# Loading x, the tables and the positions from ScalarE's DMA queue instead of SyncE's

## The chip, the core and the metric

The kernel runs on one core of a Trainium2 chip. Times are device microseconds (us) of that core; lower is better. TensorE is PE, VectorE is DVE, ScalarE is ACT, GpSimd is POOL, SyncE is SP. In the profile, PEld is PE's weight load, and SPq stands for transfers that SP issues.

## What is computed

Two layers of an encoder over 256 tokens of width 1024, all in float32. Each layer has a mixer sub-layer and an expert sub-layer, each behind an RMS norm that is scaled and shifted by a vector computed from the conditioning input c:

```python
cond = jax.nn.silu(c)
for l in range(DEPTH):
    mod = cond @ w_ada[l] + b_ada[l]
    sh1, sc1, gt1, sh2, sc2, gt2 = jnp.split(mod[:, None, :], 6, axis=-1)
    h = rms_norm(x, g_norm1[l]) * (1 + sc1) + sh1
    x = x + gt1 * hybrid_mixer(h, pos, w_in[l], ...)
    h = rms_norm(x, g_norm2[l]) * (1 + sc2) + sh2
    x = x + gt2 * hier_moe(h, w_gr[l], b_gr[l], w_er[l], b_er[l], w1[l], w3[l], w2[l])
return x
```

The mixer projects h once (`w_in`, 6944 columns), runs three kinds of attention on parts of the result, and merges them. The positions `pos` enter through rotary angles and distances between tokens. The expert sub-layer sends each token to 2 of 32 experts.

## The kernel before

**Stages.** `run` (L128) calls `plan`, which writes down the order of all weight loads, then `setup`, then the generators of the two layers: mixer, experts, mixer, experts. Instructions of an engine run in the order in which the program emits them; nothing reorders them (a manual schedule).

**Weights.** All large weights come through a stream: `plan` (L190) fills a deque of transfers, and `pump` (L73) issues the next ones from SP into buffers of 128 x 12 KB, as long as fewer than `ring` (6 here) weights are held ready and one of the 10 buffers is free in the program's order. Most weights fill a buffer with 1536 KB. The first in the stream are three parts of the first modulation matrix, `('ada', 0, 0, 0)` to `('ada', 0, 0, 2)` (called `ada 0`, `ada 1`, `ada 2` here; the third is 1024 KB), then the first halves of the first three slices of `w_in`, then `ada 3` to `ada 5`, and so on. `pump(n)` stops when n weights are held. `Tile` semaphores make a transfer wait, at issue, for an earlier transfer that used the same semaphore, and for the last reader of its buffer.

**Setup.** `setup` (L237) starts with everything that is needed early. On ACT: the load of the activation table for Exp and Ln (L240). On SP, in this order: `pk` (L242: the conditioning input, selectors, gains and an identity matrix, 98 KB), `rows` (L248: tables and short vectors, one row of 1456 bytes read for each of the 128 partitions), `ipos` (L252: positions, 1032 bytes a partition), the two tiles of x (L254, 128 rows of 4 KB each), and with `pump(2)` `ada 0` and `ada 1` (L85). Then two biases `bz` behind DVE's memsets (L258, L259), and further weights by `pump(4)`, `load_kr` (L281) and `pump()`. From `pk` ACT and DVE compute `cond` = silu(c) (L272 to L276), which every `ada` matmul reads.

**The order behind it.** The first mixer emits, for layer 0 (L1245): `setup_late` (L287), then the first step of the generator `ada_half(0)`, which is `ada 0` on PE (12 matmuls, 4 side by side on 32 columns of PE each), then `norm_x` (L481), then 16 transposes of the normed x on PE (L1254), then the rest of `ada_half(0)`: `ada 1`, `ada 2`, the bias (L435), transposed into columns (`modab`, L445). `setup_late` is work on DVE and ACT: positions to floats (L300 to L302), angles, sine and cosine (L309 to L320), gains (L326 to L334), rope tables (L343). `norm_x` sums squares of x, the left halves on ACT (L477), the right halves on DVE (L492), takes the root (L108 to L115) and scales x to `xn` (L501 on ACT, L503 on DVE). With `modab`, DVE and ACT scale the transposes and split them into two parts, `hH` and `hL` (L1281, L1286, L1287); the first projection (`in`) on PE starts on `hH`. Only then does the mixer proper begin; `ada 3` to `ada 5` and the right half of h come later in it, and the masks, a triangle and router weights are loaded from POOL's queue (L353, L354, L285).

Of the kernel before, what the change touches and what calls it, by code (L numbers as in the profile page):

```python
# [22 lines left out]
EXP_LN = 'natural_log_exp_and_others'  # L23
# [14 lines left out]
class Kern:  # L38
# [198 lines left out]
    def setup(self):  # L237

        nc, a, C = self.nc, self.a, self.const
        nc.scalar.preload_act_table_set(EXP_LN)  # L240
        pk = C('pk', [128, N_PK])
        nc.sync.dma_start(pk, a['pk'])  # L242
        self.ccol, self.sel4, self.cols = pk[:, 0:8], pk[:, 8:12], pk[:, 12:68].rearrange("p (l n) -> p l n", l=DEPTH)
        self.ident = pk[:, 68:196]
        self.identb = C('identb', [128, 128], BF)
        self.x = [self.alloc('w', [128, D], F32, 'x') for _ in range(2)]
        self.rows = C('rows', [128, N_ROW + DEPTH * 108])
        nc.sync.dma_start(self.rows, bass.AP(tensor=a['rows'].tensor, offset=a['rows'].offset,  # L248
                                             ap=[[0, 128], [1, N_ROW + DEPTH * 108]]))
        self.lrow = self.rows[:, N_ROW:].rearrange("p (l n) -> p l n", l=DEPTH)  # L250
        self.ipos = self.alloc('s', [128, 2 + T], I32, 'ipos')
        nc.sync.dma_start(self.ipos, a['pos'])  # L252
        for t in range(2):
            nc.sync.dma_start(self.x[t], a['x'][t])  # L254
        self.pump(2)
        self.bz0 = [self.alloc('s', [128, 512], F32, 'bz') for _ in range(2)]
        for h in range(2):
            nc.vector.memset(self.bz0[h], 0.0)  # L258
            nc.sync.dma_start(self.bz0[h][0:64:32], a['b_ada'][0, 0][h::2])  # L259
        self.sel2 = C('sel2', [128, 2])  # L260
        nc.vector.tensor_add(self.sel2, self.sel4[:, 0:2], self.sel4[:, 2:4])
        self.pump(4)
        self.load_kr(0)
        self.pump()
        nc.vector.tensor_copy(self.identb, self.ident)
        self.eps = C('eps', [128, 1])
        nc.vector.memset(self.eps, EPS)
        self.zero = C('zero', [128, 1])
        nc.vector.memset(self.zero, 0.0)

        t1 = self.small(8)
        nc.scalar.activation(t1, self.ccol, AF.Exp, scale=-1.0)  # L272
        nc.vector.tensor_scalar(t1, t1, 1.0, None, op0=ALU.add)
        nc.vector.reciprocal(t1, t1)
        self.cond = C('cond', [128, 8])
        nc.vector.tensor_mul(self.cond, t1, self.ccol)  # L276
        self.mod = {}
# [1636 lines left out]
```

## Time and profile before

| what | us |
|---|---|
| median of 3 runs | 1406.43 (1405.89 to 1408.21) |
| the profiled execution | 1407.64 |
| its span in the trace | 1405.5 |
| PE / DVE / ACT / POOL busy in it | 1336.0 / 683.4 / 537.3 / 187.7 |

The profile covers one execution. A span is cut into stretches by time; times in it count from the span's start. A duration of an instruction is its own; "idle before" is how long its engine stood idle ahead of it, with the work whose end released it. PE's matmuls are pipelined, so PE shows as busy while the next matmul follows; how fast it runs is read from how many matmuls fit into a time.

### The profile page before, as it was taken

Reading aid. Unit: us, or ns where it says so; the run is one execution under the profiler, and the core shown is the slowest. Engines: PE = TensorE matmul, PEld = TensorE weight load, DVE = VectorE, ACT = ScalarE, POOL = GpSimd, SP = SyncE. Lnnn points to the kernel's source line nnn. Section 1 sums busy time; section 2 is a strip of 40 time slices with the busy share of each in tenths; the row PEclk is TensorE's granted clock in tenths of the full one; section 3 lists DMA queues with packets and bytes.
Section 4 is the critical chain, followed back from the end, with each engine's and each line's share of the span. In section 5 each row is a group of like instructions: output and inputs, shape, how many; then the busy total and the mean of one; then the engine's idle time right before and its main releaser. Section 6 shows DMA issues by size and latency. Waiting matters only on the chain. (4 is left out here: it accounts for less than half of the span.)

```text
span 1405.5 us, 19475 instructions
## 1 busy us (share of the span) xinstructions
PE 1336.0 (95%) x7662; PEld 877.6 (62%) x7662; DVE 683.4 (49%) x1404; ACT 537.3 (38%) x1134; POOL 187.7 (13%) x170
## 2 busy tenths in 40 slices
PE   5999999998899999999899999999889999999997
PEld 3778787887544444444368988888764444444443
DVE  5587564767623323332256775566863233233222
ACT  4555553563422222221155555456433222222211
POOL 0002064325100000000000203540810000000000
PEclk9999999999999999999999999999899999999999
DMA  9865557267689999999994526516767999999993
GB/s 375 365 248 212 196 211 291 99 270 280 232 348 427 425 425 425 425 425 425 420 414 160 203 90 259 176 76 254 270 239 289 405 425 426 425 425 426 424 424 129
DMA packets 45215, 437.95 MB, mean 312 GB/s; under 512 B 5080, under 2 KB 5608, under 8 KB 11328
## 3 DMA queue, kind: packets, MB, share of 16 engines
q1 hardware_dynamic: 44832, 435.78, 76.5%
q8 instruction: 62, 1.02, 0.3%
q0 software_dynamic: 288, 0.89, 0.2%
q14 instruction: 33, 0.27, 0.1%
HBM read 435.59 MB, written 1.05 MB: 311 GB/s over the span
## 5 line engine op out<-in xcount | busy, mean ns | idle before, releaser
L102 PE MATMUL in<-h,hH 128*128 128x384 f32 (+1 forms) x576 | 206.1, 358 | 3.7 <-ACT hH L1286 2.5
L1631 DVE TENSOR_TENSOR O<-O,gth 64x512 f32<-64x512 f32 (+1 forms) x132 | 88.8, 673 | 241.0 <-PE O L102 240.0
L102 PE MATMUL in<-h,hL 128*128 128x384 f32 (+1 forms) x576 | 195.3, 339 | 0.1
L102 PE MATMUL in<-l,hH 128*128 128x384 f32 (+1 forms) x576 | 194.6, 338 | 0.0
L1570 ACT ACTIVATE u<-A 64x384 f32<-64x384 f32 x64 | 31.1, 486 | 301.2 <-PE A L102 301.2
L102 PEld LDWEIGHTS in<-h,hH 128*128 128x128 f32 x576 | 109.1, 189 | 29.3 <-issue 18.0
L102 PEld LDWEIGHTS in<-h,hL 128*128 128x128 f32 x576 | 108.9, 189 | 1.4 <-DVE hL L1287 1.3
L102 PEld LDWEIGHTS in<-l,hH 128*128 128x128 f32 x576 | 109.3, 190 | 0.5
L1520 ACT ACTIVATE xT<-ga,modab 128x128 f32<-128x128 f32 x256 | 92.8, 467 | 21.0 <-PE ga L102 20.9
L1637 ACT ACTIVATE Op<-O 128x1024 fp32r<-128x1024 f32 x30 | 31.7, 1057 | 138.7 <-DVE O L1631 138.7
L1571 DVE SCALAR_TENSOR_TENSOR u<-A,m,u 64x384 f32<-64x384 f32 x64 | 39.4, 616 | 89.9 <-ACT u L1570 86.2
L743 POOL TENSOR_TENSOR rot<-TB,rope 128x256 f32<-128x256 f32 x8 | 11.7, 1483 | 488.4 <-ACT UC L813 429.0
L102 PE MATMUL ga<-Poh,xp 128*128 128x256 f32 x512 | 71.7, 295 | 0.0
L1540 DVE CAST PTp<-PTe 128x256 fp32r<-128x256 bf16 x32 | 13.6, 425 | 117.4 <-PE PTe L102 117.4
L102 PE MATMUL y<-Op,PTp 128*128 128x512 f32 x240 | 70.2, 415 | 0.0
L102 PEld LDWEIGHTS ga<-Poh,xp 128*128 128x128 f32 x512 | 66.0, 198 | 5.8 <-issue 4.4
L887 ACT ACTIVATE P<-P,m 128x256 f32<-128x256 f32 (+1 forms) x48 | 27.6, 576 | 79.2 <-DVE m L945 37.1
L102 PEld LDWEIGHTS y<-Op,PTp 128*128 128x128 f32 x240 | 40.6, 188 | 21.1 <-issue 15.5
L1638 DVE TENSOR_TENSOR Op<-O,Op 128x1024 fp32r<-128x1024 f32 x30 | 36.8, 1225 | 33.8 <-ACT Op L1637 29.2
L970 POOL TENSOR_SCALAR qz<-UC,gq 128x384 f32<-128x384 f32 x16 | 22.7, 1417 | 142.7 <-PE oT L102 72.6
L973 POOL TENSOR_SCALAR bias<-dist 128x128 f32<-128x128 f32 (+1 forms) x48 | 36.1, 752 | 5.2 <-PE oT L102 1.3
L102 PE MATMUL br<-kh,oA 128*128 128x512 f32 x96 | 31.3, 401 | 0.0
(845 smaller groups left out, 2532.3 us busy)
## 6 DMA issues: line engine op xcount, KB each, us to landing
piece<-in_w_e SPq DMA_DIRECT2D x12, 512.0 KB, 4.1
w('ada', 0, 0, 0)_4_90<-in_w_ada SPq DMA_DIRECT2D x1, 1536.0 KB, 9.5
w('ada', 0, 0, 1)_5_92<-in_w_ada SPq DMA_DIRECT2D x1, 1536.0 KB
w('in', 0, 0)_9_104<-in_w_in SPq DMA_DIRECT2D x2, 768.0 KB, 16.4
w('in', 0, 1)_10_108<-in_w_in SPq DMA_DIRECT2D x2, 768.0 KB, 16.3
w('in', 0, 2)_11_110<-in_w_in SPq DMA_DIRECT2D x2, 768.0 KB, 12.2
w('ada', 0, 0, 3)_18_194<-in_w_ada SPq DMA_DIRECT2D x1, 1536.0 KB
w('ada', 0, 0, 4)_35_250<-in_w_ada SPq DMA_DIRECT2D x1, 1536.0 KB
```

The source lines that it names most:

```text
L102: self.nc.tensor.matmul(out, lhsT, rhs, start=start, stop=stop)
L743: g.tensor_mul(t[i], x, tab[:, i, :, None, :].to_broadcast([128, 2, nh, 16]))
L887: nc.scalar.activation(dst, src, AF.Exp, bias=mx_neg[:, i:i + 1], scale=1.0, accum_out=sm[:, i:i + 1])
L970: nc.gpsimd.tensor_scalar(qz, M['qd'][:, pr::2, t * 128:t * 128 + 128], self.gq[:, l, 1 + hh:2 + hh], None, op0=ALU.mult)
L973: nc.gpsimd.tensor_scalar(bias[:, lo:hi], self.dist[:, t, 256 + lo:256 + hi], -DIL_SLOPE[g][h], None, op0=ALU.mult)
L1520: nc.scalar.activation(dst, src, AF.Identity, scale=a2[:, kt:kt + 1], bias=s2[:, kt:kt + 1])
L1540: V.tensor_copy(PT[p], pv)
L1570: nc.scalar.activation(u[b:b + 64], A[c:c + 64, :384], AF.Silu)
L1571: V.scalar_tensor_tensor(u[b:b + 64], A[b:b + 64, :384], GC[e // 2][b:b + 64, e % 2:e % 2 + 1], u[b:b + 64], op0=ALU.mult, op1=ALU.mult)
L1631: V.tensor_mul(O[e // 2][b:b + 64, 512 * h + c:512 * h + c + n], o[c][p, :n], gt[p, c:c + n])
L1637: nc.scalar.activation(hi, whole, AF.Copy)
L1638: V.tensor_sub(lo, whole, hi)
```

## The change

The four transfers of x, `rows` and `ipos` are issued by ACT instead of SP, x first. `pump(2)`, the first two weights, stands directly behind `pk` on SP. The table load of ACT moves behind its four transfers.

```diff
     def setup(self):
 
         nc, a, C = self.nc, self.a, self.const
-        nc.scalar.preload_act_table_set(EXP_LN)
         pk = C('pk', [128, N_PK])
         nc.sync.dma_start(pk, a['pk'])
         self.ccol, self.sel4, self.cols = pk[:, 0:8], pk[:, 8:12], pk[:, 12:68].rearrange("p (l n) -> p l n", l=DEPTH)
         self.ident = pk[:, 68:196]
         self.identb = C('identb', [128, 128], BF)
         self.x = [self.alloc('w', [128, D], F32, 'x') for _ in range(2)]
+        for t in range(2):
+            nc.scalar.dma_start(self.x[t], a['x'][t])
+        self.pump(2)
         self.rows = C('rows', [128, N_ROW + DEPTH * 108])
-        nc.sync.dma_start(self.rows, bass.AP(tensor=a['rows'].tensor, offset=a['rows'].offset,
+        nc.scalar.dma_start(self.rows, bass.AP(tensor=a['rows'].tensor, offset=a['rows'].offset,
                                              ap=[[0, 128], [1, N_ROW + DEPTH * 108]]))
         self.lrow = self.rows[:, N_ROW:].rearrange("p (l n) -> p l n", l=DEPTH)
         self.ipos = self.alloc('s', [128, 2 + T], I32, 'ipos')
-        nc.sync.dma_start(self.ipos, a['pos'])
-        for t in range(2):
-            nc.sync.dma_start(self.x[t], a['x'][t])
-        self.pump(2)
+        nc.scalar.dma_start(self.ipos, a['pos'])
+        nc.scalar.preload_act_table_set(EXP_LN)
         self.bz0 = [self.alloc('s', [128, 512], F32, 'bz') for _ in range(2)]
```

## Rows read from the trace of the kernel before

**Rows 1.** The page, its first line.

```profile
span 1405.5 us, 19475 instructions
```

**Rows 2.** Busy time by stretch: its length, engines (instructions), granted clock, DMA, GB/s.

```profile
0.00:25.57 25.57, 10.05 (x56) 4.53 (x56) 13.99 (x72) 9.80 (x18) 0.36 (x5) 0.98 0.91 359
...
60.00:420.00 360.00, 345.38 (x2006) 269.57 (x2007) 231.31 (x498) 171.69 (x360) 93.48 (x82) 0.98 0.62 237
420.00:735.00 315.00, 304.51 (x1752) 149.16 (x1749) 100.56 (x170) 85.19 (x186) 0.00 (x0) 0.99 1.01 425
```

**Rows 3.** Waits of SP's queue, 60 to 420: total, times, longest.

```profile
SPq L85 <- DVE l L584: 104.6, 9, 19.9
SPq L85 <- PE ada L102: 60.1, 11, 14.6
```

**Rows 4.** Timeline of the start-up: start, us, engine, line, what [idle before, releaser].

```profile
6.07 0.17 DVE L300 TENSOR_SCALAR ci<-ipos 128x2 int32<-128x2 int32 x1 [2.42 <-DMA ipos<-in_pos]
...
12.68 0.68 DVE L492 SCALAR_TENSOR_TENSOR junk<-x 128x512 f32<-128x512 f32 x1
...
12.71 3.63 PE L102 MATMUL ada<-w('ada', 0, 0, 0)_4_90,cond 128*32 128x512 f32 x12 [12.71 <-DMA w('ada', 0, 0, 0)_4_90<-in_w_ada]
...
16.31 0.18 PEld L1254 LDWEIGHTS trx<-pk,xn 128*128 128x128 f32 x1 [1.70 <-DVE xn L503]
...
18.94 1.48 PE L102 MATMUL ada<-w('ada', 0, 0, 1)_5_92,cond 128*32 128x512 f32 x10
...
25.57 0.69 PE L102 MATMUL in<-h,hH 128*128 128x384 f32 x1 [2.02 <-ACT hH L1286]
```

**Rows 5.** The same timeline: what ACT and SP's queue start in front of that.

```profile
0.73 1.28 ACT L240 ACT_TABLE_LOAD   x1 [0.73 <-PEq L1902]
...
1.65 0.43 SPq L252 DMA_DIRECT2D ipos<-in_pos  x1
...
2.80 0.21 ACT L272 ACTIVATE m<-pk 128x8 f32<-128x8 f32 x1 [0.78 <-DMA pk<-in_pk]
...
3.08 0.44 SPq L85 DMA_DIRECT2D w('ada', 0, 0, 0)_4_90<-in_w_ada  x1
...
5.53 0.39 SPq L85 DMA_DIRECT2D w('ada', 0, 0, 2)_8_102<-in_w_ada  x1
```

**Rows 6.** Transfers issued 0 to 60: count, KB each, us from issue to landing.

```profile
w('ada', 0, 0, 0)_4_90<-in_w_ada SPq DMA_DIRECT2D x1, 1536.0 KB, 9.5
w('ada', 0, 0, 1)_5_92<-in_w_ada SPq DMA_DIRECT2D x1, 1536.0 KB
...
x<-in_x SPq DMA_DIRECT2D x2, 512.0 KB, 6.0
w('ada', 0, 0, 2)_8_102<-in_w_ada SPq DMA_DIRECT2D x1, 1024.0 KB, 13.2
...
rows<-in_rows SPq DMA_DIRECT2D x1, 182.0 KB, 3.6
...
ipos<-in_pos SPq DMA_DIRECT2D x1, 129.0 KB, 4.4
...
pk<-in_pk SPq DMA_DIRECT2D x1, 98.0 KB
```

**Rows 7.** DMA queues, 48 to 53.5: packets, MB, share (q1 SP, q0 POOL).

```profile
q1 hardware_dynamic: 157, 1.73, 78.1%
q0 software_dynamic: 152, 0.50, 22.7%
```

**Rows 8.** Busy time by stretch, columns as in rows 2: the transfers' first stretches.

```profile
2.00:7.20 5.20, 0.00 (x0) 0.00 (x0) 1.85 (x13) 1.51 (x3) 0.00 (x0) 1.00 0.86 279
7.20:16.30 9.10, 3.58 (x12) 0.67 (x12) 7.50 (x51) 4.11 (x10) 0.00 (x0) 1.00 1.01 416
```

**Rows 9.** PE's rate: transposes `trx` by stretch, `ada 3` (groups, 37 to 39.2), first projection.

```profile
16.30:17.62 1.32, 1.31 (x6) 1.10 (x7) 0.00 (x0) 0.00 (x0) 1.00 0.99 417
17.62:18.94 1.32, 1.32 (x12) 1.15 (x11) 0.33 (x1) 0.00 (x0) 1.00 0.99 407
...
L102 PE MATMUL ada<-w('ada', 0, 0, 3)_18_194,cond 128*32 128x512 f32 x12 | 1.9, 600 | 0.0
...
25.57:31.34 5.77, 5.77 (x18) 5.47 (x19) 4.90 (x9) 5.33 (x10) 0.00 (x0) 0.50 1.00 422
```

## The prediction

> **What bounds the kernel now.** I began with the page for the span [rows 1] and then cut the span into stretches [rows 2]: PE works nearly without a gap from 25.57 us to the end, and 25.57 us at the front are a start-up in which it works for only 10.05. In the mixer stage (60 to 420) the DMA engines move 237 GB/s, and the waits of SP's queue say why: it holds a weight back until DVE or PE has released a buffer [rows 3]. In the expert stage that follows PE and the DMA engines are both full, at 425 GB/s [rows 2], on weights whose buffers came free in the same way. So nothing behind the start-up runs on a timetable of its own: what comes later at 25.57 us comes later at the end, by the same amount, and what comes earlier likewise.
>
> The question is therefore which chain ends last in the start-up. The timeline gives two [rows 4]. One is the weight `ada 0`: PE starts on it at 12.71, when it lands, and its 12 matmuls take 3.63, to 16.34. The other starts at the positions: DVE's L300 waits for `ipos` until 6.07; behind it, in program order, stands all of `setup_late` (angles, gains, rope tables) up to 12.68, where DVE first touches x (L492). The norm follows, and the transposes start at 16.31, released by DVE's `xn`. The two chains meet within 0.03 us. Behind them PE runs in order: 16 transposes, `ada 1` and `ada 2` from 18.94, and the first projection at 25.57. DVE shows no idle time in front of L492: **the x chain is the positions' landing plus 10.24 us of fixed work**, and it is the one that the change moves later.
>
> **The change, part by part.**
>
> *The weights.* `ada 0` is issued at 3.08 now, behind pk, rows, ipos and two x [rows 5]. Afterwards it is SP's second transfer, at about 1.2. If it shares the DMA engines evenly with x, pk, both x tiles and `ada 0` are 98 + 1024 + 1536 = 2658 KB [rows 6], 2.72 MB, at 416 GB/s [rows 8] 6.5 us; from 2.0, where the transfers begin, it lands near 8.6 to 9.0. PE does its 12 matmuls some 3.8 us earlier. Worth: 0, because the transposes behind them on PE wait for `xn`, and the weights' chain had no more than its own 0.03 us to give.
>
> *x.* It lands 6.0 us after its issue, and DVE first reads it at 12.68 [rows 4, 6]. An earlier x is worth 0: DVE and ACT come to it only after the positions' work.
>
> *Table load and the four issues on ACT.* Four issues of some 0.43 us stand ahead of a table load of 1.28 [rows 5], so the Exp of L272 moves from 2.80 to about 4.0, by when pk has landed too, now sharing with x. `cond` follows a few short instructions later, about 5; its first reader is `ada 0` on PE, at 8.6 or later. Worth 0, hidden by that transfer; without this cover it would cost the 1.2 by which the Exp is later. SP saves four issues; its later ones (bz, `ada 2` now issued at 5.53) come earlier, and no queue of POOL is touched.
>
> *The positions.* This is the term that counts. Before, they were third in the only queue in use and landed in 4.4 us [rows 5, 6]. Now they are fourth in ACT's queue, and SP's queue is full of weights beside it. What two queues do to each other is seen later in this trace, where POOL loads the masks and tables beside SP's weights: between 48 and 53.5 us the one queue got 152 packets through and the other 157, though SP's carried 1.73 MB and POOL's 0.50 [rows 7]. **They take turns packet by packet, whatever their size.** All these transfers (but bz) cover 128 partitions with one row each, so they have equally many packets, and the turns pair them: pk with x 0, `ada 0` with x 1, `ada 1` with rows, `ada 2` with ipos. When ipos has had its last turn, all eight are nearly through: 98 + 1536 + 1536 + 1024 + 1024 + 182 + 129 = 5529 KB, 5.66 MB [rows 6]; at 416 GB/s 13.6 us, from 2.0 to 15.6, and a little for the slower first microsecond: 16.0. That is 9.9 later than 6.07.
>
> The bounds of it: ACT's queue served ahead of SP's would bring the positions at 2.0 + 1433 KB / 416 GB/s = 5.5 (0.5 earlier); shares equal by bytes at 2.0 + 6.8 = 8.8 (2.7 later: 98 + 2 x 1335 KB); and if the early stretch were as slow as it is now (279 GB/s, 2.0 to 7.2) the same set would be through when it is now, with `ada 2` at 5.53 + 13.2 = 18.7 (12.7 later) [rows 5, 6, 8]. I take 16.0: the row with two queues side by side is the nearest.
>
> *What else moves.* The transposes then start at 16.31 + 9.9 = 26.2. PE has been idle since its `ada 0` ended near 12.6. The first work after an idle start runs at half rate here: 12 `ada 0` matmuls in 3.63 us, the same 12 of `ada 3` in 1.9 [rows 4, 9]; and of the transposes, 6 fit into the first 1.32 us and 12 into the next [rows 9]. The granted clock prints 1.00 over both, so I go by the durations. Before, `ada 0` paid for this; afterwards the transposes and one or two of the five groups of `ada 1` and `ada 2` do. PE ran at full rate from about 17.6, 4.9 us after its first work at 12.71. At six to 1.32 us all 16 transposes take 3.5 us instead of 2.64: +0.8. That leaves 1.4 us of slow `ada` work, two groups of four matmuls; three such groups cost 1.7 more when slow, the last one's run-out included, so some 0.4 each: another 0.8. Together **+1.6**, with 0 and +2.9 (all five groups slow) as ends.
>
> The first projection now starts at a granted clock of 0.50, the 1.2 GHz level, which lasts from 25.57 to 31.34 [rows 9] and follows an idle PE, its last 2.02 us spent on ACT's `hH` [rows 4]. That gap moves along, so I leave the low stretch where it is relative to the work: 0. If it stayed away, 18 matmuls would take half of 5.77: -2.9.
>
> The sum: 9.9 + 1.6 + 0 = +11.5 us. The profiled execution took 1407.64, its span is 1405.5; from there it gives 1419.1. The median of the runs shown is 1.2 lower, 1406.43, so the forecast is **1417.9 us**, slower by 0.8%.
>
> **The rivals.**
>
> *One line for both queues.* The change does not do what it says if transfers from ACT and SP are served in the order of their issue: then ipos comes behind x, rows and both first weights, 4505 KB, 4.61 MB: 2.0 + 11.1 = 13.1, 7.0 later. Against it: the two queues of [rows 7]. It gives 1413.4 to 1415.0, by the clock term. 0.10.
>
> *Shares by bytes.* Positions 2.7 later, with 0 to 1.6 of clock: 1409.1 to 1410.7. Against it are again the equal packet counts. 0.07.
>
> *Only the issue time is saved.* SP starts the weights 1.9 us sooner, the positions keep their time, since ACT's short queue passes. The x chain is then unmoved and the sum is 0: 1406.4, at best 0.5 less. The Trainium skill, DMA: Bandwidth & Descriptors, section Issuing engines are not separate DMA queues, says that transfers from several issuing engines interleave on the same 16 DMA engines and that using several saves only the time of the issue; by that rule the sum would be this one. The trace agrees with the interleaving [rows 7]; that a short transfer loses nothing by it, no run here shows. For it: ACT's queue holds only 1335 KB. Against it: nothing in the trace lets a queue pass. 0.09.
>
> *Faster.* ACT's queue ahead of SP's, positions at 5.5, and PE, with `ada 0` done by 12.5, no longer in the low-clock stretch at 25.57: -0.5 - 2.9 = -3.4, 1403.0. It decides only if the positions land before 6.07; past that each microsecond costs one. The low stretch might go, but ipos behind a megabyte of x must also not be later. 0.03.
>
> **How the numbers follow.** Turns by packet carry 0.71. Their own range is 1414 to 1421: the -2.9 and +2.9 of the clock, and the 18.7, not all at once. The range reaches down over the single line and the byte shares: 1409 to 1421, leaving out the unmoved and the faster case (0.12) and a little above. A measurement here tells about 0.2%, 2.8 us, from no change. Slower by more: the packet turns, the single line and most of the byte shares, 0.87; within: the unmoved case and the rest, 0.10; faster: 0.03.
>
> **What would show it.** Right: DVE's L300 waits for ipos until 15 to 17; transposes 10.2 us behind it; `ada 0` on PE at 8.5 to 9, then a PE idle of over 10 us ended by `xn`; the first projection at 36 to 38; all stretches behind as long as now. Wrong: L300 starting before 9, or the transposes waiting for a weight instead of `xn`; a first projection late and an end that is not, which would mean slack behind the start-up that I did not see; a start-up as forecast with the transposes at full rate, which takes 1.6 out of the sum.

## The result, and the profile after

The changed kernel takes 1421.45 us (median of 5 runs, 1419.45 to 1422.15), against 1406.45 for the kernel before (5 runs): a ratio of 1.0102, 95% interval 1.0088 to 1.0115. It is slower by 15.0 us. The forecast was 11.5 slower, 1417.9; the measured median lies 0.45 us above the upper end of the range (1421.0).

The page of the changed kernel: its span and its two queues. `q10` is ACT's, new; `q1` is SP's.

```profile
span 1419.4 us, 19475 instructions
...
q1 hardware_dynamic: 44256, 434.41, 75.6%
...
q10 hardware_dynamic: 576, 1.37, 0.3%
```

The span is 13.9 us longer than in [rows 1]. The timeline of its start-up answers to [rows 4]: start, duration, engine, line, what, and in brackets the idle time before it with what ended it.

```profile
9.88 3.63 PE L102 MATMUL ada<-w('ada', 0, 0, 0)_3_85,cond 128*32 128x512 f32 x12 [9.88 <-DMA w('ada', 0, 0, 0)_3_85<-in_w_ada]
...
17.86 0.17 DVE L300 TENSOR_SCALAR ci<-ipos 128x2 int32<-128x2 int32 x1 [12.53 <-DMA ipos<-in_pos]
...
24.47 0.69 DVE L492 SCALAR_TENSOR_TENSOR junk<-x 128x512 f32<-128x512 f32 x1
...
28.09 0.18 PEld L1254 LDWEIGHTS trx<-pk,xn 128*128 128x128 f32 x1 [16.32 <-DVE xn L503]
28.10 3.80 PE L1254 MATMUL trx<-pk,xn 128*128 128x128 f32 x16 [14.59 <-DVE xn L503]
...
31.83 1.48 PE L102 MATMUL ada<-w('ada', 0, 0, 1)_4_87,cond 128*32 128x512 f32 x10
...
38.46 0.64 PE L102 MATMUL in<-h,hH 128*128 128x384 f32 x1 [2.02 <-ACT hH L1286]
```

The first weights come 2.8 us earlier (9.88 for 12.71). PE uses them at once and then stands idle for 14.59 us, since the transposes wait for `xn`. The positions come 11.8 us later (17.86 for 6.07), and the transposes as much (28.09 for 16.31). The waits of the first 60 us (engine, line, waited for: total, times, longest) name the same two places:

```profile
PE trx L1254 <- DVE xn L503: 14.6, 1, 14.6
...
DVE ci L300 <- DMA ipos<-in_pos: 12.5, 1, 12.5
```

The transfers issued from 0 to 60 us, with size and time from issue to landing, beside [rows 6]:

```profile
w('ada', 0, 0, 0)_3_85<-in_w_ada SPq DMA_DIRECT2D x1, 1536.0 KB, 8.6
...
w('ada', 0, 0, 2)_8_102<-in_w_ada SPq DMA_DIRECT2D x1, 1024.0 KB, 12.4
...
rows<-in_rows ACTq DMA_DIRECT2D x1, 182.0 KB, 13.3
...
ipos<-in_pos ACTq DMA_DIRECT2D x1, 129.0 KB, 15.7
```

`ada 2` was issued at 5.38 and `ipos` at 2.15: both landed at 17.8. The positions, 129 KB, needed 15.7 us where they had needed 4.4. The turns of the two queues can be counted: packets, MB and share from 4.5 to 9.8 us, and from 2.0 until the positions have landed.

```profile
q1 hardware_dynamic: 153, 1.68, 76.2%
q10 hardware_dynamic: 150, 0.51, 24.8%
...
DMA packets 1198, 6.02 MB, mean 381 GB/s; under 512 B 132, under 2 KB 494, under 8 KB 814
...
q1 hardware_dynamic: 623, 4.66, 73.9%
q10 hardware_dynamic: 575, 1.36, 25.1%
```

Where the 13.9 us arise along the kernel is read by pairing PE's 7662 matmuls of both traces in their order: 11.8 us at the first transpose, 12.9 at `ada 1`, 11.9 once the first projection runs at full rate, 13.1 after the end of layer 0's mixer (350 us), 13.5 from 380 us, 13.9 at the end. Between the jumps nothing moves, but for half a microsecond at 699 us that is made up at once. Busy time by stretch, of the changed kernel (columns as in [rows 2]): the projection's slow start, the end of the mixer, and the expert stage.

```profile
38.46:42.00 3.54, 3.54 (x11) 3.23 (x12) 2.67 (x5) 3.54 (x7) 0.00 (x0) 0.52 0.99 418
339.20:347.80 8.60, 8.11 (x35) 7.82 (x36) 8.60 (x11) 3.09 (x5) 8.60 (x6) 0.50 0.69 243
...
434.00:749.00 315.00, 304.50 (x1750) 149.50 (x1747) 101.05 (x171) 85.68 (x186) 0.00 (x0) 0.99 1.01 425
```

The expert stage is unchanged against [rows 2], at 425 GB/s. The small jumps are stretches at the 1.2 GHz level of PE's clock that come out shorter or longer: the one at the first projection ends after some 3.5 us instead of 5.77 [rows 9], the one at the mixer's end lasts longer than before, where it was this:

```profile
328.50:335.40 6.90, 6.90 (x31) 6.61 (x31) 6.90 (x8) 2.89 (x5) 6.90 (x6) 0.52 0.77 253
```

### The profile page after: what moved, and what is told of

It reads as the page before. It is cut to its first block, busy times and chain, and to the rows that moved or that the text cites. A ratio compares the mean times of both kernels' runs of the same rounds, so it can differ in the third digit from the quotient of the medians.

```text
span 1419.4 us, 19475 instructions
## 1 busy us (share of the span) xinstructions
PE 1338.1 (94%) x7662; PEld 879.0 (62%) x7662; DVE 683.4 (48%) x1404; ACT 537.2 (38%) x1134; POOL 187.7 (13%) x170
## 5 line engine op out<-in xcount | busy, mean ns | idle before, releaser
L743 POOL TENSOR_TENSOR rot<-TB,rope 128x256 f32<-128x256 f32 x8 | 11.7, 1486 | 488.8 <-ACT UC L813 429.4
L1540 DVE CAST PTp<-PTe 128x256 fp32r<-128x256 bf16 x32 | 13.6, 426 | 118.0 <-PE PTe L102 118.0
L102 PEld LDWEIGHTS y<-Op,PTp 128*128 128x128 f32 x240 | 40.6, 188 | 21.0 <-issue 15.5
```

The lines of the kernel that those rows point to most:

```text
L102: self.nc.tensor.matmul(out, lhsT, rhs, start=start, stop=stop)
L1540: V.tensor_copy(PT[p], pv)
```

## The experiments

The theory: two queues take turns packet by packet, so the n-th transfer of ACT lands with the n-th of SP; the positions land last of ACT's four; and the transposes follow their landing by a fixed 10.2 us of DVE's program. The rivals: shares by bytes; the second queue as such; the weights' place in front.

**ACT's queue in another order.**

```diff
+        nc.scalar.dma_start(self.ipos, a['pos'])
+        nc.scalar.dma_start(self.rows, ...)
         for t in range(2):
             nc.scalar.dma_start(self.x[t], a['x'][t])
         self.pump(2)
...
-        nc.scalar.dma_start(self.rows, ...)
...
-        nc.scalar.dma_start(self.ipos, a['pos'])
```

> The changed kernel with ACT's queue in another order: positions, rows, x 0, x 1. Theory (the two queues take turns packet by packet, so the n-th transfer of ACT lands with the n-th of SP): positions land with pk near 4.5 us, rows with ada 0 near 9, x 0 with ada 1 near 13.5, x 1 with ada 2 near 17.5. Now x 1 is last: transposes at 20 to 21 instead of 28.1, first projection near 30, time 1410 to 1412. Rival (shares by bytes): all four of ACT's transfers are through by about 9, transposes near 16.3, time near 1406. Rival (the weights moved to the front of SP's queue cost the time, whatever ACT's order): transposes stay near 28 and the time near 1421.

Its timeline, at the first readers of the positions, the tables, the second x tile, and the transposes:

```profile
4.70 0.16 DVE L300 TENSOR_SCALAR ci<-ipos 128x2 int32<-128x2 int32 x1
...
9.64 0.37 DVE L309 TENSOR_SCALAR ang<-rows,m 128x16 f32<-128x16 f32 x2 [3.59 <-DMA rows<-in_rows]
...
17.96 0.69 DVE L492 SCALAR_TENSOR_TENSOR junk<-x 128x512 f32<-128x512 f32 x1 [2.42 <-DMA x<-in_x]
...
20.97 0.18 PEld L1254 LDWEIGHTS trx<-pk,xn 128*128 128x128 f32 x1 [10.14 <-DVE xn L503]
```

The four landings are the theory's, within 0.8 us: by 4.7, 9.6, 14.3 (ACT's first read of x 0) and 18.0. Whatever stands last in ACT's queue comes near 18, be it 129 KB of positions or 512 KB of x. Shares by bytes are out, and so is the weights' place alone, for it did not change. The time was 1415.19, ratio 1.0052 (1.0037 to 1.0068), 3 us above the forecast's upper end: the transposes and the first `ada` groups ran slowly behind the idle PE (the shift grows from 4.7 to 6.1 us there), and stretches at the low clock later added 1.4 in all.

**The same order of transfers in one queue.**

```diff
-            nc.scalar.dma_start(self.x[t], a['x'][t])
+            nc.sync.dma_start(self.x[t], a['x'][t])
...
-        nc.scalar.dma_start(self.rows, ...)
+        nc.sync.dma_start(self.rows, ...)
...
-        nc.scalar.dma_start(self.ipos, a['pos'])
+        nc.sync.dma_start(self.ipos, a['pos'])
```

> The changed kernel's order of transfers, all of them issued by SP: pk, x, ada 0, ada 1, rows, positions. Theory (turns between two queues are what delays the positions, on top of the order): in one line they come behind 4505 KB, 13 to 14 us instead of 17.9; transposes near 24, first projection near 34.5, time 1415 to 1417. Rival (the second queue plays no part, the order of issue alone does): positions again near 17.9 and the time near 1421.

The positions' landing in its timeline, a stretch of its DMA traffic (columns as in [rows 2]), and all of its packets from 1 to 17 us:

```profile
16.99 0.17 DVE L300 TENSOR_SCALAR ci<-ipos 128x2 int32<-128x2 int32 x1 [13.29 <-DMA ipos<-in_pos]
```

```profile
14.00:16.00 2.00, 0.29 (x2) 0.00 (x0) 0.00 (x0) 0.00 (x0) 0.00 (x0) 1.00 0.80 258
...
DMA packets 1108, 5.34 MB, mean 334 GB/s; under 512 B 119, under 2 KB 503, under 8 KB 766
```

A miss of the theory's price, and an instructive one. The positions landed only 0.9 us sooner than with two queues, and the time was 1420.93, ratio 1.0091 (1.0075 to 1.0106). So the second queue itself is worth at most 0.9 us at the landing; even that is not certain, since the changed kernel's transfers, left as they are in two kernels below, landed the positions at 17.2 and 17.0. The two times are not told apart; **what costs is that the small transfers stand behind megabytes of weights**, and turns between two queues are just another way of standing behind them. My 13 to 14 us went wrong in two terms. The rate was too high: at 334 GB/s from 1.0 on, the 4.61 MB up to the positions' end would be through by 14.8 (321 from 2 to 7 us, 258 in the stretch shown). And the other 0.73 MB that had moved by 17 belong to transfers issued behind the positions, 2.2 us at that rate. Why those got through before the positions had landed, no row shows.

**Only the small ones on ACT's queue**, x in front of the weights on SP's.

```diff
-            nc.scalar.dma_start(self.x[t], a['x'][t])
+            nc.sync.dma_start(self.x[t], a['x'][t])
         self.pump(2)
...
-        nc.scalar.dma_start(self.rows, ...)
...
         nc.scalar.dma_start(self.ipos, a['pos'])
+        nc.scalar.dma_start(self.rows, ...)
```

> Only positions and rows on ACT's queue, x in front of the weights on SP's. Theory: positions land with pk near 4 to 5 us, rows with x 0 near 5.5, ada 0 near 10; both chains are 1 to 2.5 us earlier than before the change: transposes at 14 to 15.5, first projection 23.5 to 25, time 1404 to 1406. Rival (a second queue always delays what shares it): positions later than 6.07 and the time above 1407.

Its timeline, at the first readers of the positions and of the tables, at `ada 0`, and at the transposes:

```profile
4.37 0.16 DVE L300 TENSOR_SCALAR ci<-ipos 128x2 int32<-128x2 int32 x1
...
7.02 0.37 DVE L309 TENSOR_SCALAR ang<-rows,m 128x16 f32<-128x16 f32 x2 [1.29 <-DMA rows<-in_rows]
...
12.46 3.63 PE L102 MATMUL ada<-w('ada', 0, 0, 0)_3_85,cond 128*32 128x512 f32 x12 [12.46 <-DVE rope L343]
...
16.02 2.41 PE L1254 MATMUL trx<-pk,xn 128*128 128x128 f32 x16
```

The whole loss is gone with the small transfers paired to pk and x 0: 1407.39 against 1407.70 for the kernel before in the same runs, ratio 0.9996 (0.9987 to 1.0005). The positions came at 4.4 as expected, but there was no gain, for two reasons. `ada 0` still started at 12.46, only 0.25 us sooner than in [rows 4], though it was issued 0.9 us earlier: it landed 10.2 us after its issue at 2.17 (the profile names a work of DVE that ended at the same moment). The bytes ahead of it were the same, and the first microseconds were as slow as before (232 GB/s from 2 to 6 here, 234 there). And the x chain now waited for the tables: DVE stood idle until 7.02, so that chain gained under half a microsecond of the 1.7. The transposes came at 16.02, as `ada 0`'s matmuls ended, 0.3 us earlier than before.

**Only x on ACT's queue**; rows and positions on SP, directly behind pk.

```diff
-        self.pump(2)
...
-        nc.scalar.dma_start(self.rows, ...)
+        nc.sync.dma_start(self.rows, ...)
...
-        nc.scalar.dma_start(self.ipos, a['pos'])
+        nc.sync.dma_start(self.ipos, a['pos'])
+        self.pump(2)
```

> Only x on ACT's queue; rows and positions back on SP, directly behind pk, the weights behind them. Theory (what costs is the small transfers' place behind weights, not the second queue and not x in it): positions land at 5 to 7, ada 0 near 12, transposes near 16, first projection at 25 to 26, time 1405.5 to 1408, as before the change. Rival (x beside the weights in a second queue costs time): first projection later than 27, time above 1409.

Its timeline, at the positions and the transposes:

```profile
8.14 0.17 DVE L300 TENSOR_SCALAR ci<-ipos 128x2 int32<-128x2 int32 x1 [2.66 <-DMA ipos<-in_pos]
...
18.37 3.86 PE L1254 MATMUL trx<-pk,xn 128*128 128x128 f32 x16 [2.82 <-DVE xn L503]
```

1411.12, ratio 1.0037 (1.0024 to 1.0051): slower than expected, and by time and projection the rival's case, since x in a second queue did cost time. The rows keep the theory, though: the small transfers now took turns with x's packets, the positions landed 2.07 us later than before, and the transposes started 2.06 later. The rest is PE's rate: `ada 0` ended by 15.5, PE stood idle for 2.82, the 16 transposes took 3.86 us instead of 2.70, `ada 1` was slow too, and the projection began at 29.86, 4.3 late. A small lateness of x costs about twice itself here.

Four kernels in which the positions are the last that DVE's work in front of the transposes waits for, all on the same line:

| kernel | positions (L300) | transposes | between |
|---|---|---|---|
| before | 6.07 | 16.31 | 10.24 |
| x alone on ACT | 8.14 | 18.37 | 10.23 |
| one queue | 16.99 | 27.21 | 10.22 |
| changed | 17.86 | 28.09 | 10.23 |

**The norm of x in front of the work on the positions**, with the changed kernel's transfers.

```diff
         if l == 0:
-            late, distances = self.setup_late()
             next(g)
         xn, _ = self.norm_x('xn', self.ss if l else None, self.fill if l else None)
+        if l == 0:
+            late, distances = self.setup_late()
```

> The changed kernel's transfers, untouched; only the order of emission changes: the norm of x stands in front of the work on the positions. Theory (late positions delay x through DVE's program order, not because x needs them): transposes right behind ada 0, at 13.5 to 14 us instead of 28.1, though the positions land at 17.9 as before. The bias sum of the modulation still stands behind the positions' DVE work, so it comes at 25 to 26 and the first projection at 28.5 to 30, not 38.5; time 1409 to 1412. Rival (the projection is late because weights or x are late in the two queues): transposes stay behind 25 and the time near 1421.

Its timeline: the transposes, the positions, the bias sum of the modulation, the first projection.

```profile
13.82 1.97 PE L1255 MATMUL trx<-pk,xn 128*128 128x128 f32 x16
...
17.18 0.17 DVE L300 TENSOR_SCALAR ci<-ipos 128x2 int32<-128x2 int32 x1 [4.91 <-DMA ipos<-in_pos]
...
24.40 0.68 DVE L435 TENSOR_TENSOR modrow<-ada,bz 128x512 f32<-128x512 f32 x1
...
29.01 0.69 PE L102 MATMUL in<-h,hH 128*128 128x384 f32 x1 [2.01 <-ACT hH L1287]
```

x never needed the positions: the transposes are at 13.82, 14.3 us earlier than in the changed kernel, with the positions nearly as late as there (17.18 for 17.86). Now the bias sum (L435) stands behind the positions' work, and the projection comes at 29.01, in the expected interval; the time, 1412.57, is 0.6 above its own, ratio 1.0044 (1.0029 to 1.0059).

**Both repairs**: small transfers alone on ACT's queue, and the norm first (the edits of the third and the fifth experiment together).

> The same queues as the kernel with only positions and rows on ACT, and the norm of x emitted in front of the work on the positions. Theory (in the order of DVE's work lies the coupling of x to the positions): x no longer waits for them; ada 0 on PE near 10, transposes right behind it near 13.5, the positions' 6.6 us of DVE work under ada 1 and ada 2, whose landing (16 to 17) ends last; first projection near 22, time 1402 to 1404. Rival (the positions' work is needed in front of the first projection anyway): no gain over the kernel without the new order, 1404 to 1406.

Its timeline, at `ada 0`:

```profile
12.44 3.63 PE L102 MATMUL ada<-w('ada', 0, 0, 0)_3_85,cond 128*32 128x512 f32 x12 [12.44 <-DVE pi L301]
```

1406.55 against 1407.70, ratio 0.9993 (0.9984 to 1.0002): no difference, the rival's case. `ada 0` at 12.44 holds everything, as in the third experiment.

**The positions' work moved behind the start of the projection**, with the changed kernel's transfers.

```diff
         if l == 0:
-            late, distances = self.setup_late()
             next(g)
...
-            dist = distances()
-            for n in range(4):
-                later(15 + 4 * n, lambda: next(dist, None))
...
             if l == 0 and i == 5:
+                late, distances = self.setup_late()
+                dist = distances()
+                for n in range(4):
+                    later(10 + 4 * n, lambda: next(dist, None))
```

> The changed kernel's transfers, with the norm of x first and all work on the positions emitted only at the sixth step of the first projection, where DVE and ACT stand idle. Theory: nothing in front of the first projection waits for the positions; the chain is ada 0 (9.9), transposes 13.5, ada 2 landing at 17.8, first projection at 22 to 23.5, time 1402.5 to 1405, faster than both kernels. Rival (the positions' work moves its 6.6 us to where it stops PE): first projection early, and a gap of PE of several us behind it; time 1406 or more.

Its timeline: `ada 2` on PE, the first projection, the first work on the positions.

```profile
17.96 1.07 PE L102 MATMUL ada<-w('ada', 0, 0, 2)_8_102,cond 128*32 128x512 f32 x8 [0.35 <-DMA w('ada', 0, 0, 2)_8_102<-in_w_ada]
...
22.91 0.69 PE L102 MATMUL in<-h,hH 128*128 128x384 f32 x1 [2.02 <-ACT hH L1285]
...
29.76 0.16 DVE L300 TENSOR_SCALAR ci<-ipos 128x2 int32<-128x2 int32 x1
```

With the same transfers that cost 15 us, the projection now starts 2.66 us earlier than in the kernel before [rows 4], behind the landing of `ada 2`. PE shows no new gap at 29.76. The time was 1405.60 against 1406.80, ratio 0.9991 (0.9982 to 1.0000): a gain at the edge of what can be told, 0.6 us above the expected interval, and less than the 2.66 us by which the projection is earlier.

**The same, with rows and positions loaded behind the first weights.**

```diff
-        nc.scalar.dma_start(self.rows, ...)
-        nc.scalar.dma_start(self.ipos, a['pos'])
...
         self.load_kr(0)
         self.pump()
+        nc.sync.dma_start(self.rows, ...)
+        nc.sync.dma_start(self.ipos, a['pos'])
```

> As the kernel with the late work on the positions, and rows and positions loaded behind the first weights on SP instead of beside them. Theory (these two small transfers take DMA time from ada 1 and ada 2: the stretch 12 to 14.5 us in the changed kernel moved 242 to 331 GB/s): ada 2 lands at 15.5 to 16.5, first projection at 20.5 to 22, time 1401 to 1403. Rival (they cost only their 311 KB, 0.75 us): 0.5 to 1 us less than with them in front, 1402 to 1404.

Its timeline: the end of `ada 2` on PE and the first projection.

```profile
16.92 1.20 PE L102 MATMUL ada<-w('ada', 0, 0, 2)_8_100,cond 128*32 128x512 f32 x6
...
21.98 0.44 PE L102 MATMUL in<-h,hH 128*128 128x384 f32 x1 [2.02 <-ACT hH L1285]
```

`ada 2` no longer makes PE wait, and the projection starts at 21.98, 3.6 us earlier than before. 1404.05 against 1406.80, ratio 0.9980 (0.9971 to 0.9989): the only version that beats both kernels clear of noise. It lies 1 us above the expected interval.

**The tables stored once per partition** in memory, so that the 128 packets of `rows` read 128 places instead of one. First in the changed kernel:

```diff
-    a['rows'] = np.concatenate([rows, lrows.reshape(-1)])
+    a['rows'] = np.ascontiguousarray(np.broadcast_to(np.concatenate([rows, lrows.reshape(-1)]), (128, N_ROW + L * 108)))
...
-        nc.scalar.dma_start(self.rows, bass.AP(...))
+        nc.scalar.dma_start(self.rows, a['rows'])
```

> The changed kernel, with the rows table stored once for each partition in memory (as the positions already are), so that its 128 packets read 128 places instead of one. Bytes, order and queues stay. Theory (the positions came 1.9 us later than forecast because the DMA engines move only 242 to 331 GB/s while rows is read, 12 to 14.5 us): no dip, positions land at 15.7 to 16.5, first projection at 36.5 to 37.5, time 1419 to 1420.5. Rival (the dip has another cause, a start-up or a semaphore): positions stay at 17.5 to 18 and the time at 1420.5 to 1422.

Busy time by stretch: the changed kernel (two lines); the kernel with the norm first and the one with the positions' work moved, which both have the changed kernel's transfers (one line each); then this kernel, from 12 to 14.5 us and at its transposes.

```profile
12.00:14.50 2.50, 1.51 (x4) 0.00 (x0) 0.00 (x0) 0.00 (x0) 0.00 (x0) 1.00 0.88 258
14.50:17.80 3.30, 0.00 (x0) 0.00 (x0) 0.00 (x0) 0.00 (x0) 0.00 (x0) 1.00 1.01 419
...
12.00:14.50 2.50, 2.50 (x14) 0.89 (x9) 0.27 (x1) 2.01 (x3) 0.00 (x0) 1.00 0.91 341
...
12.00:14.50 2.50, 2.50 (x11) 0.88 (x7) 0.00 (x0) 0.31 (x1) 0.00 (x0) 1.00 0.92 355
...
12.00:14.50 2.50, 1.50 (x4) 0.00 (x0) 0.00 (x0) 0.00 (x0) 0.00 (x0) 1.00 0.98 406
...
27.39:31.18 3.79, 3.79 (x17) 3.25 (x17) 1.03 (x2) 0.79 (x2) 0.00 (x0) 0.50 0.99 412
```

With one row shared by all partitions, the stretch from 12 to 14.5 us moved 258, 341 and 355 GB/s in three executions; with a row for each partition the dip is gone (406), and from 2 to 17 us 400 GB/s were moved instead of 377 to 379. So reading one place 128 times slows the traffic. What that is worth at the landing is not shown: the positions came at 17.16, between what the theory and the rival expected and 0.7 us sooner than in the changed kernel, but the two kernels with the shared row had them at 17.18 and 17.02.

The projection, expected at 36.5 to 37.5, came at 39.03, later than in the changed kernel. The transposes were 0.7 us earlier (27.39, again 10.2 behind the positions), but PE ran slowly for longer: ten matmuls of `ada 1` took 2.70 us instead of 1.48. The granted clock over these transposes is 0.50, the 1.2 GHz level. The time was 1420.16, ratio 1.0096 (1.0080 to 1.0112), not told apart from the changed kernel.

Then in the kernel before, with the transfer on SP:

> The kernel before the change, with the same table stored once for each partition. Theory: the stretch 3 to 5 us, 211 GB/s with rows in it, runs faster; positions land near 5 and ada 0 near 11.5 instead of 12.7, both chains about 1 us earlier, time 1405 to 1406. Rival (the slow stretch is the transfers' start, whatever they read): both within 0.4 us of before, time 1406 to 1407.5.

The positions landed at 4.25, 1.8 us sooner, and `ada 0` started at 12.02, 0.7 us sooner. The stretch from 3 to 5 us hardly changed: 227 GB/s for 211, so the shared row is not what makes the start slow. In the profiled execution the projection started 1.6 us sooner, but over 11 runs the time was 1406.71 against 1407.07, ratio 0.9997 (0.9988 to 1.0006): not told apart from no change, as the rival expected.

## Why the prediction was right, and where it was off

- **Which chain ends last.** Right. The x chain follows the positions by 10.2 us wherever they are the last that it waits for; the distance is longer where x, the tables or PE's `ada 0` came later (16.3 with ACT's queue turned, 11.7 with the small transfers alone on it). That DVE's order ties x to the positions was shown by turning that order. And an earlier `ada 0` (9.88, forecast 8.6 to 9.0) was worth nothing: PE's wait for it became a wait of 14.59 for `xn`.
- **How two queues share.** Right: ACT's four transfers landed with SP's first four, shown in the changed kernel and with ACT's order turned, and counted in packets: from 4.5 to 9.8 us 150 of ACT's queue to 153 of SP's, with 0.51 and 1.68 MB. The interleaving on one set of engines that the Trainium skill states (DMA: Bandwidth & Descriptors, Issuing engines are not separate DMA queues) is what the trace shows; the rival built on it, that only issue time changes, missed what the interleaving does to a short transfer.
- **The positions' landing** was the mis-sized term: 16.0 forecast, 17.86 measured, 11.8 us late instead of 9.9. Two parts make up nearly all of the 1.9 us. From 2.0 to 17.8 the mean was 381 GB/s where I put 416: 5.66 MB take 14.9 us by that instead of 13.6, and I had allowed 0.4 for it, so 0.9. And 6.02 MB had moved, not 5.66: SP's queue carried 4.66 MB, 0.37 more than its four transfers of the sum, another 0.9. How late the positions come is itself not sharp: 17.0 to 17.9 in three executions of the same transfers.
- **PE's rate.** Forecast +1.6: 0.8 on the transposes and 0.8 on `ada`. Measured 1.1 on the transposes (3.80 for 2.70) and nothing on `ada`, which ran at full rate from its first group (10 matmuls in 1.48, as in [rows 4]). The split is chance: from the first transpose to the projection it was 9.26 us before, 10.37 in the changed kernel and with one queue, 10.67 with ACT's queue turned, 11.49 with x alone on ACT and 11.64 with a table row for each partition, so +1.1 to +2.4 for the same work behind an idle PE. The forecast's 1.6 lies among them. The granted clock that printed 1.00 over slow work in the forecast's rows is 0.50 over equally slow transposes of that last kernel.
- **The low-clock stretches.** I put 0, by moving the one at the projection along unchanged. It became shorter (12.9 to 11.9 of shift), and later ones longer (11.9 to 13.9): +1.0 in all. Together 11.8 + 1.1 + 1.0 is the 13.9 of the span. Why the later ones changed is not shown; the kernel before alone spreads from 1405.3 to 1409.1 us over its runs, and its runs at a mean granted clock of 0.986 all lie below 1406.4.
- **From one execution to the median.** The forecast took off 1.2 us, by which the profiled execution before (1407.64) lay above its median. The profiled execution of the changed kernel is its median (1421.45), so nothing was to be taken off, and that is the step from 13.9 (the spans) to 15.0 (the medians). It is as large as most of the misses above.
- **Delay passes to the end.** Right in the traces: behind the first 50 us the shift shrinks nowhere for good, through the expert stage at 425 GB/s too. In the medians it passes less exactly: over the eleven kernels the change of the time lies 0.4 below to 2.3 above that of the projection's start.
- **The rivals.** *One line for both queues* was priced at 1413.4 to 1415.0; the kernel that is just that took 1420.93. It was mis-sized by the same two parts as the forecast, rate and bytes of later transfers. So time could not have told it from the forecast, and the order is the cause, not the number of queues. *Faster* named the right place for a gain, but not the way to it: the repair was in DVE's order.

## What to carry to other kernels

Moving a short transfer is judged by what stands in front of it and beside it, not by its size: 129 KB took 15.7 us once it was the fourth of its queue beside three large ones. Before paying for an earlier transfer, look at which engine's program order ties its consumers to other data; here a new order of emission took back the whole loss of 15 us with the same transfers (ratio 0.9991 to the kernel before, 0.9982 to 1.0000). Two chains that meet within 0.03 us give nothing for speeding up one.

## What I had not expected of the hardware

A transfer that reads the same 1456 bytes for 128 partitions slows everything beside it: 258, 341 and 355 GB/s from 12 to 14.5 us in three executions, 406 when each partition has its own copy. The first microseconds of transfers are slower than the 416 GB/s of [rows 8] in every order, from 2 to 7.2 us: 279 before, 283 with the small transfers alone on ACT, 321 in one queue, 371 in the changed kernel. They are slowest where small transfers go first, and a row for each partition changes little (292 in the kernel before); the cause stays open. And behind only 2.8 us of idle PE the 16 transposes of the start-up took 3.86 us instead of 2.70.
